# Seven block products in place of eight for two double groups of a feed-forward input

## The chip, the cores and the metric

The kernel runs on one core of one Trainium2 chip. The metric is the time of one execution on the device, in microseconds (us). TensorE (PE) multiplies, VectorE (DVE), ScalarE (ACT) and GpSimd (POOL) work elementwise, SyncE (SP) issues most transfers from HBM.

## The reference

One decoder layer on 256 tokens of 1,024 features, in float32. Before the part that is changed come an attention branch, a recurrent branch, their merge, and cross-attention to 256 memory tokens. What is changed is the last step:

```python
hn = rmsnorm(h, norm_ffn_g[l])
gu = hn @ w_ffn_in[l]                       # 1024 x 5632
h = h + (jax.nn.silu(gu[..., :FFN_HIDDEN]) * gu[..., FFN_HIDDEN:]) @ w_ffn_out[l]   # FFN_HIDDEN = 2816
return rmsnorm(h, final_norm_g)
```

## The kernel before

**Three matmuls for one.** Every float32 operand is cut in two: `hi`, a copy rounded to the format fp32r, and `lo`, the rest. A product is `hi*hi + hi*lo + lo*hi`, three matmuls on TensorE (`mm3t`, lines 238 to 240), added up in PSUM.

**Weight units.** All weights lie in HBM as units of 128 x 2048 numbers (1 MB), in the order `ORDER` in which they are used. `prep` loads a unit into one of two `raw` buffers, ScalarE copies it to `hi` (line 194), and `lo = raw - hi` (line 198) is made by VectorE (1,152 columns) and GpSimd (896 columns, `POOL_COLS`), in two pieces. There are three `hi` and three `lo` buffers, and `nxt` prepares two units ahead of the one in use.

**The feed-forward part.** `FFN_HIDDEN` is worked on in 11 groups of 256 units. A group has two input units `("I", j, kh)`, for the lower and the upper half `kh` of the 1,024 inner features, each with 256 gate columns and 256 value columns, and one output unit `("O", j)`. The order is I, I of group j, then O of group j - 1. For an I unit, `ffn_in` runs for both groups `t` of 128 tokens: four slices of 128 features times three matmuls of 512 columns, so 12 matmuls for each `t`, into the PSUM bank `psi`. After both halves `kh`, `gate` makes silu(gate) * value, where ScalarE and VectorE also apply the token's normalising factor `r`; `turn_hid` transposes the result (four transposes, `hidT`, line 1099) and cuts it (`hid`, lines 285 and 286); an O unit is 24 matmuls into four PSUM banks `acc` that stay for the whole part.

**The turn of h.** While the stage before it (`wo_part`, the output of the cross-attention) still runs, `turn_h2` transposes one quarter of `h` (128 tokens by 512 features) at a time (`h2T`, line 1064), applies the gain (VectorE, line 1066) and cuts it (ScalarE line 1067, GpSimd line 1068). It is turned unscaled; the factor `r` is known later and is used in `gate`. The last quarter is turned between the two `t` of the first I unit, which does not read that quarter yet.

**Who sets the order.** TensorE's instructions stand in the order in which the program writes them. Those of the other engines are put in order by a scheduler when the program is built; the order of the built program is fixed, each engine works strictly through its own, and semaphores hold it where an operand or a buffer is not ready.

Of the kernel before, what the change touches and what calls it, by code (L numbers as in the profile page):

```python
# [24 lines left out]
EPS = 1e-6  # L25
NEG = -1e30
LEAD = 2
POOL_COLS = 896
# [12 lines left out]
V_MIX, V_X, V_MEM, V_FFN, V_HG, V_L0, V_L1 = (8 * i for i in range(7))  # L41


def plan():
    order = []

    def tgroup(name, base):
        return [("T", name, base + c * 512, kh) for c in range(2) for kh in range(2)]

    order += [("T", "w_in", 4096 + c * 512, kh) for kh in range(2) for c in range(2)]  # L50
    order += [("F", "w_in", 3 * 1024 + c * 256) for c in range(4)]
    for base in (5, 2, 0, 1, 6):
        order += tgroup("w_in", base * 1024)
    order += tgroup("w_in", 8 * 1024) + tgroup("w_in", 7 * 1024)
    order += tgroup("w_br_hgrn", 0) + tgroup("w_br_attn", 0)
    order += tgroup("w_out", 0)
    order += [("F", "wkv_x", c * 256) for c in range(4)]
    order += tgroup("wkv_x", 1024)[:2]
    order += [("F", "wq_x", c * 256) for c in range(4)]
    order += tgroup("wkv_x", 1024)[2:]  # L60
    order += tgroup("wo_x", 0)
    for j in range(NF // 2):
        order += [("I", j, 0), ("I", j, 1)]
        if j:
            order.append(("O", j - 1))
    order.append(("O", NF // 2 - 1))
    return order


ORDER = plan()  # L70


def lay(ws):
# [39 lines left out]
def bc(ap, n, axis):  # L113
    shape = list(ap.shape)
    shape.insert(axis, n)
    return ap.unsqueeze(axis).to_broadcast(shape)


def build(tc, A, out):
    nc = tc.nc  # L120
    V, SC, G, PE, SY = nc.vector, nc.scalar, nc.gpsimd, nc.tensor, nc.sync
    with ExitStack() as ctx:
# [3 lines left out]
        cp = pool("cp", 1)  # L126
        wr, wh, wl = pool("wr", 2), pool("wh", 3), pool("wl", 3)
# [114 lines left out]
        def by_k(w, k):  # L242
            return tuple(t.rearrange("p (k c) -> p k c", k=k) for t in w)
# [276 lines left out]
        w = by_k(nxt(), 4)  # L520
# [394 lines left out]
        def add_h(t, c, ps, scale, ssq):  # L915
            d = H[:, t, c * 512:(c + 1) * 512]
            if scale is None:
                V.tensor_tensor(d, ps, d, op=ALU.add)
            else:
                V.scalar_tensor_tensor(d, ps, scale, d, op0=ALU.mult, op1=ALU.add)  # L920
            j = t2b("hjunk")
            SC.activation(j, d, AF.Square, accum_out=ssq[:, t, c:c + 1])

        def rstd2(ssq, name):
            s = small("s2", [2])
            V.tensor_tensor(s, ssq[:, :, 0], ssq[:, :, 1], op=ALU.add)
            return rstd_of(s, name)
# [124 lines left out]
        gfin = big("B4", "gfin", (128, 1024))  # L1052
        SY.dma_start(gfin, A["gfin"].to_broadcast([128, 1024]))
        H2 = big("P2", "H2", (128, 2, 8, 256), F32R)
        h2h, h2l = H2[:, 0], H2[:, 1]
        def wo_part(ps, t, c, kh):
            t_part(ps, wo[2 * c + kh], (oxh, oxl), t, kh)

        def turn_h2(t, c):
            ks, ts = slice(4 * c, 4 * c + 4), slice(t * 128, (t + 1) * 128)  # L1060
            bk = bank("h2T", (128, 4, 128))
            for j in range(4):
                k = 4 * c + j
                PE.transpose(bk[:, j], H[:, t, k * 128:(k + 1) * 128], ident)
            g = t2("h2g", (128, 4, 128))
            V.tensor_tensor(g, bk, bc(gv[:, V_FFN + 4 * c:V_FFN + 4 * c + 4], 128, 2), op=ALU.mult)
            SC.activation(h2h[:, ks, ts], g, AF.Copy)
            G.tensor_tensor(h2l[:, ks, ts], g, h2h[:, ks, ts].bitcast(F32), op=ALU.subtract)

        todo = None  # L1070
        for t in range(2):
            for c in range(2):
                ps = mm.tile([128, 512], F32, name="pso", tag="mm")
                wo_part(ps, t, c, 0)
                if todo:
                    turn_h2(*todo)
                wo_part(ps, t, c, 1)
                add_h(t, c, ps, None, ssq2)
                todo = (t, c)


        ring = ("B7", "B14", "B10", "B11", "B12", "B6")
        X2 = (h2h, h2l)
        hid, acc, two, psi, hm = {}, {}, {}, {}, {}

        def gate(o, t):
            r, ps = two["r"][:, t:t + 1], psi.pop((o, t))
            g = t2("fg", (128, 256))
            SC.activation(g, ps[:, 0:256], AF.Silu, scale=r)  # L1089
            u = t2b("fu", (128, 256))  # L1090
            V.scalar_tensor_tensor(u, ps[:, 256:512], r, g, op0=ALU.mult, op1=ALU.mult)  # L1091
            hm[o, t] = u

        def turn_hid(o):
            bk = mm.tile([128, 2, 256], F32, name="hidT", tag="mm")
            for t in range(2):
                u = hm.pop((o, t))
                for j in range(2):
                    PE.transpose(bk[:, j, t * 128:(t + 1) * 128], u[:, j * 128:(j + 1) * 128], ident)
            hd = big(ring[o % 6], "hid", (128, 2, 2, 256), F32R)  # L1100
            split(bk, hd[:, 0], hd[:, 1])
            hid[o] = hd

        def ffn_in(o, kh, t, w):
            if kh == 0:
                psi[o, t] = mm.tile([128, 512], F32, name="psi", tag="mm")
            t_part(psi[o, t], w, X2, t, kh)
# [11 lines left out]
        def ffn_out(o):  # L1119
            w = by_k(nxt(), 2)  # L1120
            for t in range(2):
                for c in range(2):
                    out_part(o, w, t, c)
# [20 lines left out]
        wa = by_k(nxt(), 2)  # L1144
        wb = by_k(nxt(), 2)
        out_part(n - 1, wa, 0, 0)
        turn_hid(n)
        out_part(n - 1, wa, 0, 1)
# [8 lines left out]


        ssq3 = cp.tile([128, 5], F32, name="ssq3")
        hg3 = {i: big(ring[j], "hg3", (128, 512)) for j, i in enumerate(((0, 0), (0, 1), (1, 0)))}  # L1160
# [95 lines left out]
```

## Time and profile before

| | us |
|---|---|
| median of three executions | 625.4 (624.79 to 625.51) |
| profiled execution, its own time | 625.08 |
| span in its profile, first to last instruction | 623.1 |
| mean granted TensorE clock | 0.998 |
| start of the feed-forward's first matmul | about 431 |
| last matmul | 616.4 |

The span begins with the first instruction and ends with the last; the execution's own time has some 2 us more around it. A row of the timeline gives start and duration in us, the engine, the line of the kernel, the operation, the tiles (output<-inputs) and the count; in square brackets is the idle time of the engine before it and what ended it. A row of the chain of waits gives start, the time until the next piece of the chain, and the instruction. A row of groups gives count | busy time in us, mean duration in ns | idle time before, and what ended it. A row of windows gives the stretch, its length, the busy time and count of TensorE's matmuls, its weight loads, VectorE, ScalarE and GpSimd, then the granted clock, the DMA engines' busy share and GB/s.

### The profile page before, as it was taken

What the parts mean: (1) busy time and instruction counts of PE and PEld (TensorE: products, weight loads), DVE (VectorE), ACT (ScalarE), POOL (GpSimd) and SP (SyncE); (2) the same over time, 40 slices, a digit from 0 to 9 for tenths busy, and PEclk for the clock granted to TensorE, in tenths of its full rate; (3) what the DMA queues carried; (4) which work ended last, traced back from release to release, by engine and by line L of the source; (5) the groups of instructions that cost most, each with busy time, mean ns of one, the idle gap of its engine ahead of it and who ended that gap; (6) DMA issues with size and microseconds to landing.
All of it is one profiled execution on the core that took longest, in us unless ns stands there. A gap on an engine that the chain in (4) does not pass through costs nothing.

```text
span 623.1 us, 8546 instructions
## 1 busy us (share of the span) xinstructions
PE 615.1 (99%) x3153; PEld 513.7 (82%) x3153; DVE 395.6 (63%) x691; ACT 334.1 (54%) x550; POOL 371.5 (60%) x296
## 2 busy tenths in 40 slices
PE   8999999999999999999999999999999999999995
PEld 7888888888877877778888888888888888888884
DVE  7589888979776875748846456754444444444433
ACT  7785554234376866727547556644543344434432
POOL 3888744556544564356857876656655665566553
PEclk9999999999999999999999999999999999999999
DMA  8754553334433333545454544453354455455511
GB/s 346 288 197 149 203 202 136 136 135 147 191 137 135 136 136 136 203 174 191 145 213 189 187 176 178 143 196 135 136 180 175 187 202 184 177 184 198 204 68 68
DMA packets 16890, 107.53 MB, mean 173 GB/s; under 512 B 2000, under 2 KB 2640, under 8 KB 4560
## 3 DMA queue, kind: packets, MB, share of 16 engines
q1 hardware_dynamic: 16128, 106.14, 46.9%
q10 hardware_dynamic: 720, 0.84, 0.4%
q8 instruction: 25, 0.41, 0.3%
q14 instruction: 17, 0.14, 0.1%
HBM read 105.92 MB, written 1.05 MB: 172 GB/s over the span
## 4 chain that ended last, share of the span: by engine, by line
PE 98%; DVE 0%; POOL 0%; issue 0%; POOLq 0%; DVEq 0%
PE pst L238 13%; PE pst L240 13%; PE pst L239 13%; PE psf L259 7%; PE psi L238 6%; PE psi L240 6%; PE psi L239 6%; PE psf L260 4%; PE acc L240 3%; PE acc L238 3%; PE acc L239 3%; PE lp L613 2%; PE psg L514 1%; PE pso L238 1%; PE pso L240 1%; PE pso L239 1%
## 5 line engine op out<-in xcount | busy, mean ns | idle before, releaser
L198 POOL TENSOR_TENSOR lo<-raw,hi 128x448 fp32r<-128x448 f32 x172 | 272.0, 1597 | 181.4 <-ACT hi L194 178.4
L194 ACT ACTIVATE hi<-raw 128x1024 fp32r<-128x1024 f32 (+1 forms) x194 | 196.2, 1037 | 161.1 <-PE pst L240 58.2
L198 DVE TENSOR_TENSOR lo<-raw,hi 128x576 fp32r<-128x576 f32 (+2 forms) x194 | 197.8, 1024 | 127.9 <-ACT hi L194 126.1
L238 PE MATMUL pst<-hi,XX 128*128 128x512 f32 x224 | 90.4, 404 | 0.0
L240 PE MATMUL pst<-hi,XX 128*128 128x512 f32 x224 | 87.4, 390 | 0.0
L239 PE MATMUL pst<-lo,XX 128*128 128x512 f32 x224 | 87.3, 390 | 0.0
L238 PE MATMUL psi<-hi,H 128*128 128x512 f32 x176 | 69.6, 395 | 0.0
L240 PE MATMUL psi<-hi,H 128*128 128x512 f32 x176 | 68.7, 390 | 0.0
L239 PE MATMUL psi<-lo,H 128*128 128x512 f32 x176 | 68.5, 389 | 0.0
L240 PEld LDWEIGHTS pst<-hi,XX 128*128 128x128 f32 x224 | 42.0, 188 | 9.0
L238 PEld LDWEIGHTS pst<-hi,XX 128*128 128x128 f32 x224 | 42.1, 188 | 8.8 <-issue 0.7
L239 PEld LDWEIGHTS pst<-lo,XX 128*128 128x128 f32 x224 | 42.1, 188 | 7.9
L240 PEld LDWEIGHTS psi<-hi,H 128*128 128x128 f32 x176 | 33.0, 188 | 7.1
L239 PEld LDWEIGHTS psi<-lo,H 128*128 128x128 f32 x176 | 33.1, 188 | 6.6
L238 PEld LDWEIGHTS psi<-hi,H 128*128 128x128 f32 x176 | 33.1, 188 | 6.5
L238 PE MATMUL acc<-hi,hid 128*128 128x512 f32 x86 | 33.6, 390 | 0.0
L240 PE MATMUL acc<-hi,hid 128*128 128x512 f32 x86 | 33.5, 389 | 0.0
L239 PE MATMUL acc<-lo,hid 128*128 128x512 f32 x86 | 33.5, 389 | 0.0
L1091 DVE SCALAR_TENSOR_TENSOR fu<-psi,r_h,fg 128x256 f32<-128x256 f32 x22 | 10.6, 483 | 25.1 <-ACT fg L1089 25.1
L1089 ACT ACTIVATE fg<-psi,r_h 128x256 f32<-128x256 f32 x22 | 10.4, 475 | 29.1 <-PE psi L240 29.1
L259 PE MATMUL psf<-H,hi 128*128 128x512 f32 x64 | 22.8, 400 | 0.0
L259 PE MATMUL psf<-XX,hi 128*128 128x512 f32 x64 | 22.6, 396 | 0.0
(336 smaller groups left out, 1199.4 us busy)
## 6 DMA issues: line engine op xcount, KB each, us to landing
raw<-w SPq DMA_DIRECT2D x94, 1024.0 KB, 4.8
raw<-w SPq DMA_DIRECT2D x4, 512.0 KB, 6.5
raw<-w SPq DMA_DIRECT2D x4, 256.0 KB, 4.0
H<-xtok SPq DMA_DIRECT2D x1, 1024.0 KB, 9.6
mraw<-mT SPq DMA_DIRECT2D x1, 1024.0 KB, 4.9
xraw<-xT SPq DMA_DIRECT2D x1, 512.0 KB, 6.5
gfin<-gfin SPq DMA_DIRECT2D x1, 512.0 KB, 3.7
out<-H SPq DMA_DIRECT2D x2, 256.0 KB, 2.0
```

What stands on the lines that cost most here:

```text
L194: SC.activation(hi[:, a], raw[:, a], AF.Copy)
L198: eng.tensor_tensor(lo[:, b], raw[:, b], hi[:, b].bitcast(F32), op=ALU.subtract)
L238: PE.matmul(ps, xh, h, start=first, stop=False)
L239: PE.matmul(ps, xh, l, start=False, stop=False)
L240: PE.matmul(ps, xl, h, start=False, stop=last)
L259: PE.matmul(ps, w[0][:, k, a], X2[:, :, k], start=k == 0, stop=False)
L260: PE.matmul(ps[:, 0], w[1][:, k, a], X2[:, 0, k], start=False, stop=k == 7)
L514: PE.matmul(pss[c][t], z[:, k, t * 128:(t + 1) * 128], ws[c][0][:, k], start=z is Xh and k == 0, stop=False)
L613: PE.matmul(ps[:, j], KS[:, a0 + j], QQ[:, a0 + j], start=True, stop=True)
L1089: SC.activation(g, ps[:, 0:256], AF.Silu, scale=r)
L1091: V.scalar_tensor_tensor(u, ps[:, 256:512], r, g, op0=ALU.mult, op1=ALU.mult)
```

## The change

Only the feed-forward part is changed.

**Seven products.** Groups 3 and 4, and groups 7 and 8, are each taken together. For such a pair q, q + 1 the input product is a 2 x 2 product of blocks: tokens in two halves `t`, inner features in two halves `kh`, and two groups. Eight block products (12 matmuls each) become seven, P1 to P7, in a form after Strassen and Winograd. Sums of token blocks (`token_sums`, tile `SS`) are made once; sums of weight blocks (`load_blocks`, `block`) are made on VectorE by `both`, in two halves of 1,024 columns, in the loaded tiles `b11`, `b12`, `b21` and `b22`, and are then cut like any unit. P1, P6, P5 and P3 add up in one PSUM bank; copies kept on the way (`keep`, ScalarE) are added to other banks by `whole` (VectorE).

**One block sum by a transfer.** For the pair 7, 8 (`BY_DMA`) ScalarE negates block 12, and a transfer issued by GpSimd adds block 22 to it from HBM.

**The order.** `FFN_PLAN` gives 39 units in place of 33: I units of groups 0, 1, 2 and O0; then P1, P2, O1, P6, P7, P5, O2, P3, P4; I units of 5 and 6, O3; then P1, P2, O4, P6, P7, O5, P5, O6, P3, P4; I of 9, O7, I of 10, O8, O9, O10. `prep_u(n + 3)` prepares three units ahead, with a fourth pair of buffers (`px`) beside the three; `raw` stays at two. From the third unit on a unit is cut in one piece. `TURNS` says at which unit `turn_hid` stands, `LOADS` where the four blocks of a pair are asked for.

**The turn.** `h` is now scaled by its factor before it is transposed (`rstd_h2`, `hn`), so `gate` no longer multiplies by `r`. The quarters of `t` = 0 are turned between the two halves of the last `wo_part`. The first four I units run for `t` = 0 alone; then both quarters of `t` = 1 are turned, and the same four units run for `t` = 1.

```diff
+SEVEN = ("P1", "P2", "P6", "P7", "P5", "P3", "P4")
...
+    out = two(0) + two(1) + two(2) + [("O", 0)]
+    out += seven(3, P2=[1], P5=[2]) + two(5) + two(6) + [("O", 3)]
+    out += seven(7, P2=[4], P7=[5], P5=[6])
+    out += two(9) + [("O", 7)] + two(10) + [("O", 8)]
+    return out + [("O", 9), ("O", 10)]
...
+BY_DMA = (7,)
+LOADS = {0: (3,), 14: (7,)}
+TURNS = {4: (0,), 7: (1,), 11: (2,), 18: (3,), 21: (4,), 24: (5,), 26: (6,), 32: (7,), 34: (8,), 35: (9,)}
...
+        def halve(raw, n):
+            if n % 4 == 3:
+                hi, lo = px[:, 0:2048], px[:, 2048:4096]
+            else:
+                hi = wh.tile([128, 2048], F32R, name="hi", tag="hi")
+                lo = wl.tile([128, 2048], F32R, name="lo", tag="lo")
+            pieces = 2 if n < 2 else 1
+            w = 2048 // pieces
+            for c in range(pieces):
+                a = slice(c * w, (c + 1) * w)
+                SC.activation(hi[:, a], raw[:, a], AF.Copy)
+                cut = (c + 1) * w - POOL_COLS // pieces
+                V.tensor_tensor(lo[:, c * w:cut], raw[:, c * w:cut], hi[:, c * w:cut].bitcast(F32), op=ALU.subtract)
+                G.tensor_tensor(lo[:, cut:a.stop], raw[:, cut:a.stop], hi[:, cut:a.stop].bitcast(F32),
+                                op=ALU.subtract)
+            return hi, lo
+
+        def both(out, x, y, op):
+            for i in range(2):
+                a = slice(1024 * i, 1024 * i + 1024)
+                V.tensor_tensor(out[:, a], x[:, a], y[:, a], op=op)
+
+        def load_blocks(q):
+            blk.clear()
+            for key, tag, c in (("22", "B12", (q + 1, 1)), ("12", "B6", (q + 1, 0)),
+                                ("11", "B10", (q, 0)), ("21", "B11", (q, 1))):
+                blk[key] = big(tag, "b" + key, (128, 2048))
+                SY.dma_start(blk[key], A["w"][where[("I",) + c]])
+            if q in BY_DMA:
+                SC.activation(blk["12"], blk["12"], AF.Copy, scale=-1.0)
+                G.dma_start(blk["12"], A["w"][where["I", q + 1, 1]], accum_op=ALU.add)
+            else:
+                both(blk["12"], blk["22"], blk["12"], ALU.subtract)
+
+        def block(name):
+            if name == "P6":
+                both(blk["11"], blk["12"], blk["11"], ALU.add)
+            elif name == "P5":
+                both(blk["12"], blk["22"], blk["11"], ALU.subtract)
+            elif name == "P4":
+                both(blk["21"], blk["21"], blk["11"], ALU.subtract)
+            return blk[{"P1": "11", "P2": "21", "P6": "11", "P7": "12", "P5": "12", "P3": "22", "P4": "21"}[name]]
+
+        def prep_u(upto):
+            while made_u[0] <= min(upto, len(units) - 1):
...
+                if u[0] == "P":
+                    raw = block(u[2])
+                else:
+                    raw = wr.tile([128, 2048], F32, name="raw", tag="raw")
+                    SY.dma_start(raw, A["w"][where[u]])
+                pair[n] = halve(raw, n)
...
+        def product(ps, name, w, first):
+            xh, xl = tokens(name)
+            for k in range(4):
+                for i, (x, z) in enumerate(((xh, w[0]), (xh, w[1]), (xl, w[0]))):
+                    PE.matmul(ps, x[k], z[:, k], start=first and k == 0 and i == 0, stop=k == 3 and i == 2,
+                              skip_group_check=not first)
...
+        def whole(q, t, ps, key):
+            c = t2("fc")
+            V.tensor_tensor(c, ps, kept.pop(key), op=ALU.add)
+            psi[q, t] = c
+            gate(q, t)
...
-        for u in ORDER[at[0]:-2]:
-            if u[0] == "O":
-                ffn_out(u[1])
-                continue
-            _, o, kh = u
-            w = by_k(nxt(), 4)
-            for t in range(2):
-                ffn_in(o, kh, t, w)
-                if (o, kh, t) == (0, 0, 0):
-                    turn_h2(1, 1)
-                    two["r"] = rstd2(ssq2, "h2")
-                if kh == 1:
-                    gate(o, t)
-            if kh == 0 and o:
-                turn_hid(o - 1)
+        prep_u(3)
+        for n in range(4):
+            ffn_in(n, 0)
+        turn_h2(1, hn1)
+        for n in range(4):
+            for q in LOADS.get(n, ()):
+                load_blocks(q)
+            ffn_in(n, 1)
+            if n == 0:
+                token_sums()
+            prep_u(n + 4)
+        for n in range(4, len(units) - 2):
+            for q in LOADS.get(n, ()):
+                load_blocks(q)
+            prep_u(n + 3)
+            for o in TURNS.get(n, ()):
+                turn_hid(o)
+            u = units[n]
+            if u[0] == "I":
+                for t in range(2):
+                    ffn_in(n, t)
+            elif u[0] == "P":
+                ffn_product(n)
+            else:
+                ffn_out(n)
```

More of the change, by code (lines that the diff above doesn't have):

```diff
@@ L70, with ffn_plan, seven, two @@
 ORDER = plan()
+SEVEN = ("P1", "P2", "P6", "P7", "P5", "P3", "P4")
+def ffn_plan():
+    def seven(q, **after):
+        out = []
+        for p in SEVEN:
+            out.append(("P", q, p))
+            out += [("O", o) for o in after.get(p, ())]
+        return out
+    def two(j):
+        return [("I", j, 0), ("I", j, 1)]
+    out = two(0) + two(1) + two(2) + [("O", 0)]
[3 more added lines that the diff above has]
+    return out + [("O", 9), ("O", 10)]
+FFN_PLAN = ffn_plan()
+BY_DMA = (7,)
+LOADS = {0: (3,), 14: (7,)}
+TURNS = {4: (0,), 7: (1,), 11: (2,), 18: (3,), 21: (4,), 24: (5,), 26: (6,), 32: (7,), 34: (8,), 35: (9,)}
 def lay(ws):
@@ L1055, in build @@
         h2h, h2l = H2[:, 0], H2[:, 1]
+        where = {u: i for i, u in enumerate(ORDER)}
+        px = big("P1", "px", (128, 4096), F32R)
+        made_u, pair, blk = [0], {}, {}
+        def halve(raw, n):
[14 more added lines that the diff above has]
+            return hi, lo
@@ L1070, in build, with add_h2, rstd_h2 @@
-        todo = None
+        ssq2 = cp.tile([128, 4], F32, name="ssq2")
+        v2 = cp.tile([128, 2], F32, name="v2")
+        r2 = cp.tile([128, 2], F32, name="r2")
+        h2g = {}
+        def add_h2(t, c, ps):
+            d = H[:, t, c * 512:(c + 1) * 512]
+            V.tensor_tensor(d, ps, d, op=ALU.add)
+            SC.activation(t2b("hjunk"), d, AF.Square, scale=1.0 / 32.0, accum_out=ssq2[:, 2 * t + c:2 * t + c + 1])
+        def rstd_h2(t):
+            V.tensor_scalar(v2[:, t:t + 1], ssq2[:, 2 * t:2 * t + 1], ssq2[:, 2 * t + 1:2 * t + 2], EPS,
+                            op0=ALU.add, op1=ALU.add)
+            G.tensor_tensor(r2[:, t:t + 1], v2[:, t:t + 1], nhalf[:, :1], op=ALU.pow)
+            hn = []
+            for c in range(2):
+                n = t2("hn")
+                SC.activation(n, H[:, t, c * 512:(c + 1) * 512], AF.Copy, scale=r2[:, t:t + 1])
+                hn.append(n)
+            return hn
@@ new lines, in turn_h2 @@
+        def turn_h2(t, hn):
+            for c in range(2):
+                ks, ts = slice(4 * c, 4 * c + 4), slice(t * 128, (t + 1) * 128)
+                bk = bank("h2T", (128, 4, 128))
+                for j in range(4):
+                    PE.transpose(bk[:, j], hn[c][:, j * 128:(j + 1) * 128], ident)
+                g = t2("h2g", (128, 4, 128))
+                V.tensor_tensor(g, bk, bc(gv[:, V_FFN + 4 * c:V_FFN + 4 * c + 4], 128, 2), op=ALU.mult)
+                SC.activation(h2h[:, ks, ts], g, AF.Copy)
+                G.tensor_tensor(h2l[:, ks, ts], g, h2h[:, ks, ts].bitcast(F32), op=ALU.subtract)
+                h2g[t, c] = g
@@ L1071, in build @@
+        hn0 = None
         for t in range(2):
@@ L1117, in out_part, with ffn_in @@
                      (o == 0 or home is not None) and k == 0, k == 1 and o >= NF // 2 - (2 if t and c else 1))
-        def ffn_out(o):
-            w = by_k(nxt(), 2)
+        def ffn_in(n, t):
+            _, o, kh = units[n]
+            if kh == 0:
+                psi[o, t] = mm.tile([128, 512], F32, name="psi", tag="mm")
+            t_part(psi[o, t], by_k(pair[n], 4), X2, t, kh)
+            if kh == 1:
+                gate(o, t)
+        SS = big("P0", "SS", (128, 2, 4, 4, 128), F32R)
@@ new lines, in token_sums, with put @@
+        def token_sums():
+            a11, a12, a21, a22 = (h2g[t, c] for t in range(2) for c in range(2))
+            def put(i, g):
+                SC.activation(SS[:, 0, i], g, AF.Copy)
+                G.tensor_tensor(SS[:, 1, i], g, SS[:, 0, i].bitcast(F32), op=ALU.subtract)
+            V.tensor_tensor(a22, a21, a22, op=ALU.add)
+            s2 = t2("s2", (128, 4, 128))
+            V.tensor_tensor(s2, a22, a11, op=ALU.subtract)
+            put(1, s2)
+            V.tensor_tensor(a21, a11, a21, op=ALU.subtract)
+            put(2, a21)
+            put(0, a22)
+            V.tensor_tensor(a12, a12, s2, op=ALU.subtract)
+            put(3, a12)
@@ new lines, in build, with keep, ffn_product @@
+        bank_of, kept = {}, {}
+        def keep(key, ps, home):
+            SC.activation(home, ps, AF.Copy)
+            kept[key] = home
+        def whole(q, t, ps, key):
[3 more added lines that the diff above has]
+            gate(q, t)
+        def ffn_product(n):
+            _, q, name = units[n]
+            w = by_k(pair[n], 4)
+            key = {"P1": "A", "P6": "A", "P5": "A", "P3": "A", "P2": "B", "P7": "F", "P4": "F"}[name]
+            first = name in ("P1", "P2", "P7")
+            if first:
+                bank_of[key] = mm.tile([128, 512], F32, name="pq" + key, tag="mm")
+            ps = bank_of[key]
+            product(ps, name, w, first)
+            if name == "P1":
+                keep("1", ps, t2("f1"))
+            elif name == "P2":
+                whole(q, 0, ps, "1")
+            elif name == "P6":
+                keep("2", ps, gf[:, 1024:1536])
+            elif name == "P5":
+                keep("4", ps, gf[:, 1536:2048])
+                whole(q + 1, 1, bank_of["F"], "4")
+            elif name == "P3":
+                psi[q + 1, 0] = ps
+                gate(q + 1, 0)
+            elif name == "P4":
+                whole(q, 1, ps, "2")
@@ L1143, in build @@
         n = NF // 2 - 1
-        wa = by_k(nxt(), 2)
-        wb = by_k(nxt(), 2)
+        wa, wb = (by_k(pair[len(units) - 2 + i], 2) for i in range(2))
         out_part(n - 1, wa, 0, 0)
```

65 lines of the change are left out of this document (33 added, 32 removed).

## The prediction, made before the changed kernel ran

> **What bounds the kernel now.** I read the page first: the busy shares, and the shares of the chain that ended last. In these views DVE is VectorE, ACT ScalarE, POOL GpSimd, SP the queue that issues the loads.
>
> ```profile
> span 623.1 us, 8546 instructions
> PE 615.1 (99%) x3153; PEld 513.7 (82%) x3153; DVE 395.6 (63%) x691; ACT 334.1 (54%) x550; POOL 371.5 (60%) x296
> PE 98%; DVE 0%; POOL 0%; issue 0%; POOLq 0%; DVEq 0%
> ```
>
> TensorE is the chain. What a matmul is worth is its pitch in the chain of waits, not its duration in the groups (some 390 ns), since matmuls overlap:
>
> ```profile
> 448.10 0.44 PE hidT L1099 x4
> 464.89 0.44 PE hidT L1099 x4
> ```
>
> These two are one trip of the feed-forward loop apart: 16.79 us hold four transposes and 72 matmuls, so a matmul of 512 columns costs (16.79 - 0.44) / 72 = 0.227 us and a weight unit of 24 matmuls 5.45 us.
>
> Then the question is whether the weights still come fast enough. The timeline of one unit shows how ScalarE makes its upper half (`hi`) and then VectorE (576 of each 1024 columns) and GpSimd (448) the rest (`lo`):
>
> ```profile
> 471.23 2.00 ACT L194 ACTIVATE hi<-raw 128x1024 fp32r<-128x1024 f32 x2
> 472.31 0.76 DVE L198 TENSOR_TENSOR lo<-raw,hi 128x576 fp32r<-128x576 f32 x1 [0.47 <-ACT hi L194]
> 473.26 1.44 DVE L198 TENSOR_TENSOR lo<-raw,hi 128x576 fp32r<-128x576 f32 x1 [0.19 <-ACT hi L194]
> 472.36 3.36 POOL L198 TENSOR_TENSOR lo<-raw,hi 128x448 fp32r<-128x448 f32 x2 [2.88 <-ACT hi L194]
> ```
>
> The same VectorE job takes 0.76 and then 1.44 us, although both have 576 columns. The stretch at 148 us shows why:
>
> ```profile
> 148.86 0.80 DVE L581 TENSOR_TENSOR QK<-QK,Tt 128x512 f32<-128x512 f32 x1
> 149.59 1.77 DVE L583 TENSOR_TENSOR QK<-QK,Tt 128x512 f32<-128x512 f32 x1
> 151.29 2.37 DVE L198 TENSOR_TENSOR lo<-raw,hi 128x576 fp32r<-128x576 f32 x2
> 147.97 1.16 POOL L198 TENSOR_TENSOR lo<-raw,hi 128x448 fp32r<-128x448 f32 x1
> 149.08 1.74 POOL L741 TENSOR_TENSOR ra<-ra,rb__1439 128x512 f32<-128x512 f32 x1
> 150.78 1.59 POOL L198 TENSOR_TENSOR lo<-raw,hi 128x448 fp32r<-128x448 f32 x1
> 431.18 1.29 POOL L1068 TENSOR_TENSOR H<-h2g,H 128x512 fp32r<-128x512 f32 x1
> ```
>
> GpSimd's 448 columns take 1.16 us alone and its 512 columns 1.29 us. At 149.08 it begins 512 columns while VectorE is in L581, and ends at 150.82: 1.29 us after VectorE let go at about 149.5. VectorE's L583, begun at 149.59, ends at 151.36, some 0.55 us after GpSimd let go; then GpSimd, then VectorE. So an operation of VectorE with both inputs in SBUF and one of GpSimd exclude each other and **take turns**; their times add up. Operations that read PSUM do not join in:
>
> ```profile
> 146.72 1.28 POOL L741 TENSOR_TENSOR ra<-ra,rb__1421 128x512 f32<-128x512 f32 x1 [2.68 <-DVE rb__1421 L740]
> 146.74 0.69 DVE L738 TENSOR_TENSOR ra<-pst,Ct 128x512 f32<-128x512 f32 x1
> ```
>
> The Trainium skill, "SBUF — State Buffer", section "Who interferes with whom", says the same: a VectorE instruction with two SBUF inputs and a GpSimd one that reads SBUF block each other for whole instructions. It speaks against this change, which adds such operations and spreads them over less TensorE time; without the rule the sum would be the first rival's. The 0.80, 1.74, 1.77 and 1.59 above agree with it.
>
> **What it removes.** Two groups of units side by side are four weight blocks, 4 x 24 = 96 matmuls; seven block products of 12 are 84. Twice, that is 24 matmuls, and the built program has 2,202 matmuls of 512 columns in place of 2,226. Worth 24 x 0.227 = **-5.4 us**. Transposes stay as many.
>
> **Prices of the new operations.** These rows give the slopes:
>
> ```profile
> 15.84 1.21 DVE L198 TENSOR_TENSOR lo<-raw,hi 128x1024 fp32r<-128x1024 f32 x1
> L198 DVE TENSOR_TENSOR lo<-raw,hi 128x512 fp32r<-128x512 f32 x8 | 5.4, 694 | 0.6 <-ACT hi L194 0.6
> L194 ACT ACTIVATE hi<-raw 128x1024 fp32r<-128x1024 f32 x186 | 191.4, 1055 | 158.8 <-PE pst L240 58.2 <-PE psi L240 32.1 <-PE acc L240 28.1
> L194 ACT ACTIVATE hi<-raw 128x512 fp32r<-128x512 f32 x8 | 4.8, 622 | 2.4 <-DMA x0g<-x0g 1.7 <-DMA raw<-w 0.7
> L286 DVE TENSOR_TENSOR hid<-hidT,hid 128x512 fp32r<-128x512 f32 x11 | 7.5, 685 | 1.4 <-ACT hid L285 1.4
> raw<-w SPq DMA_DIRECT2D x94, 1024.0 KB, 4.8
> ```
>
> A unit is now cut in one piece. ScalarE's 2048 columns: 1.055 + 2 x (1.055 - 0.622) = 1.92 us. VectorE's 1152: 1.21 + 128 x (1.21 - 0.694)/512 = 1.34. GpSimd's 896: 1.16 + 448 x (1.29 - 1.16)/64 = 2.07, at most 2 x 1.16 = 2.32; I take 2.13. Half a block sum (1024 columns) is 1.21 on VectorE. So a unit takes 1.34 + 2.13 = 3.5 us of turns, about as before, but a product uses it up in 12 x 0.227 = 2.7 us.
>
> **The late turn.** Row group 1 of the tokens is now scaled, turned and cut after all four first units have run on group 0, and TensorE stands in its own order behind that turn. Before, the chain ran beside matmuls:
>
> ```profile
> 434.01 0.44 PE h2T L1064 x4
> 434.48 0.69 DVE L1066 TENSOR_TENSOR h2g<-h2T,gv 128x512 f32<-128x512 f32 x1 [1.25 <-PE h2T L1064]
> 435.21 0.63 ACT L1067 ACTIVATE H<-h2g 128x512 fp32r<-128x512 f32 x1 [2.38 <-DVE h2g L1066]
> 435.92 1.29 POOL L1068 TENSOR_TENSOR H<-h2g,H 128x512 fp32r<-128x512 f32 x1 [1.91 <-ACT H L1067]
> ```
>
> `hi` is there 1.83 us and `lo` 3.20 us after the first transpose. Eight transposes cover 0.88: 0.95 us of pause; two matmuls later (2.28) comes `lo`: 0.92 more. Block 12's two halves (2.4 us) stand just ahead on VectorE: 0 to 2.4, I take 0.9, since most of ten microseconds may hide them. Group 0 has the last 12 matmuls of the stage before as cover (4.06 with the transposes and three matmuls, against 3.20), less one GpSimd weight job of 2.13 if it is in front: 0 to 1.3, I take 0.9. Together **+3.7** (1.9 to 5.6).
>
> **The two rounds of seven.** The built program's order on VectorE from P1's weights on is: lo(P1), a `hid` cut, two halves of P6's block, lo(P2), two halves of P4's block, lo(O), lo(P6), a `hid` cut. So P4's block, wanted six units later, stands ahead of the `lo` of the output unit that follows P2. Its seven two-input jobs let GpSimd in between, which has lo(P1), lo(P2), lo(O), lo(P6), lo(P7) ready: 3 x 1.34 + 4 x 1.21 + 5 x 2.13 = 19.5 us to lo(O). The third matmul of O needs the `hid` cut as well, behind lo(P6): + 1.34 + 0.69 = 21.5. In round two the output unit after P7 is ready too, one turn more: 23.7.
>
> TensorE comes to that matmul 2 x 2.73 + 0.45 = 5.9 us after P1's start. How long before P1 is lo(P1) begun? Two `raw` buffers remain, and one is bound for 4.8 (landing) + 1.92 + 1.34 + 2.13 = 10.2 us, or 5.1 us per unit against 5.45 on TensorE: a lead once lost hardly returns. Ahead of round one it is lost: during the late half of the first four units (10.9 us) the turns hold two h2 cuts, four cuts and four sums of tokens (6 x 1.29 + 4 x 0.69) and unit 4: 14.0 us. I take one unit of lead: an output unit with its turn and P1's own jobs, 5.89 + 3.5 = 9.4. Pauses: 21.5 - 15.3 = **+6.2** and 23.7 - 15.3 = **+8.4**. With no lead (3.5) they are 12.1 and 14.3; with three units (over 16.8) none.
>
> Rest of each round: VectorE has five more `lo` (6.7 us), two halves of P5's block (2.4), four 512-column operations on PSUM at 0.69 (2.8) and small gates, some 13 us, and four turns of GpSimd (8.5); TensorE has five products (13.6), the next output unit and most of O (10.4), 24 us. That is close: 0 to 4 us each, I take 2: **+4**.
>
> **The accumulating transfer** puts negation on ScalarE (1.92) and a GpSimd transfer in place of two halves (2.4). The issue waits for the negation, that for a load whose buffer is freed late in round one, and GpSimd's `lo` of the I units queue behind; on SP the next `raw` stands behind two block loads. No row shows such a transfer: from -2.4 to +4.8 (a plain load's time, if GpSimd were held for all of it). I take 0, the I units having room.
>
> **The clock.** Pauses of this length may lower it:
>
> ```profile
> 1.56 3.57 PE warm L335 x15
> 5.13 2.71 PE psg L514 x8
> 8.30 0.92 PE psg L514 x4
> 616.35 0.28 PE L240 MATMUL end<-hi,hid 128*128 128x256 f32 x1
> 616.00:620.00 4.00, 0.63 (x6) 0.43 (x4) 2.51 (x7) 2.32 (x8) 1.84 (x2) 1.00 0.35 131
> 620.00:623.10 3.10, 0.00 (x0) 0.00 (x0) 0.00 (x0) 0.00 (x0) 0.00 (x0) 0.66 0.46 169
> ```
>
> 0.66 over the last 3.1 us is full speed for 1 us and half after: it fell at 621, 4.4 us after the last matmul. Recovery lasted some 5 us (eight matmuls at 0.339, later 0.23), up to 2.5 us lost; as other waits follow, I take 1 for each round: **+2** (0 to 5). The Trainium skill, "TensorE: Matmul & The Clock Gate", section "Why this matters for your kernels", warns of pauses over some 3 us, a free-running window having to be idle. By that the broken pause of round one might escape: +1.
>
> **Sum:** -5.4 + 3.7 + 6.2 + 8.4 + 4 + 2 = +18.9. The profiled execution took 625.1 (span 623.1 and 2.0 around it), the median is 625.4: **644.3 us**.
>
> **Rivals.**
> *The lead holds (faster).* If P1's jobs begin 15.6 (17.8 in round two) us ahead of it, both rounds are covered: 625.4 - 5.4 + 3.7 = 623.7; 620 if the turn is covered too. It would also come so if the big operations did not take turns. For it speaks GpSimd's idle time in this stage:
>
> ```profile
> L198 POOL TENSOR_TENSOR lo<-raw,hi 128x448 fp32r<-128x448 f32 x66 | 110.2, 1688 | 70.6 <-ACT hi L194 70.6
> ```
>
> Against it the turns and the two buffers. Chance 0.07.
> *No lead at all.* 12.1 and 14.3 in place of 6.2 and 8.4: 656, more if the accumulating transfer holds GpSimd. 0.09.
> *A middle,* half a round covered: 626.7 to 634. 0.04. About no change: 0.02. That the matmuls are not saved is excluded by the count.
>
> **Range.** The forecast has 0.78. Half a unit of lead (2.7 us) either way in each round, 5.4, and 4 for the rests below; 5.4 and the transfer's 4.8 above: 634 to 655. A measurement tells 0.2% (1.3 us) from no change. Faster 0.07, same 0.02, slower 0.78 + 0.09 + 0.04 = 0.91.
>
> **What would show it.** Right: TensorE idle only in feed-forward, longest at the output units O1 and O4 behind P2, released by VectorE's `lo`; VectorE's halves there 3.3 us long, each ending 1.2 us after GpSimd's; a pause at the late turn released by ScalarE and then GpSimd. Wrong: P1's `lo` begun over 16 us ahead; halves of 1.2 us beside busy GpSimd; a hold on GpSimd at the accumulating transfer; pauses released by DMA, which would make the loads the cause.

## The result, and the profile after

| | before | after |
|---|---|---|
| median, us | 625.31 (624.79 to 625.51, 4 runs) | 643.75 (643.51 to 645.21, 4 runs) |
| span of the profiled execution, us | 623.1 | 641.7 |
| mean granted TensorE clock | 0.998 | 0.983 |

The ratio is 1.0301 (95% interval 1.0283 to 1.0319): 18.4 us slower, where +18.9 was predicted. The total is right to 0.6 us, but not all of its terms are, and the experiments moved one of them far outside its bounds.

The page after, its first lines, the shares of the chain, and rows of groups and transfers:

```profile
span 641.7 us, 8474 instructions
PE 618.8 (96%) x3129; PEld 513.2 (80%) x3129; DVE 436.7 (68%) x690; ACT 349.9 (55%) x540; POOL 387.7 (60%) x277
PE 85%; POOL 4%; DVE 3%; issue 3%; DMA 2%; ACT 2%; POOLq 0%; DVEq 0%; ACTq 0%
...
L1108 DVE TENSOR_TENSOR b<-b,b 128x1024 f32<-128x1024 f32 x14 | 26.6, 1926 | 0.0
...
b<-w POOLq DMA_DIRECT2D x1, 1024.0 KB, 12.7
```

TensorE fell from 98% of the chain to 85%. The halves of the block sums (L1108) took 1.93 us on average (from 1.21 to 3.15), not 1.21, and the accumulating transfer 12.7 us. What TensorE waited for in the feed-forward part (us in total, times, longest):

```profile
PE acc L263 <- DVE px L1099: 5.7, 1, 5.7
PE acc L264 <- DVE hids L310: 4.3, 2, 3.3
PE psi L262 <- ACT H L1177: 2.1, 1, 2.1
PE hidT L1212 <- DVE fu L1205: 1.2, 1, 1.2
PE psi L264 <- POOL H L1178: 1.0, 2, 0.6
PE psi L262 <- DVE fu L1205: 0.3, 1, 0.3
```

The places are those foretold: VectorE's `lo` and `hid` cuts at O1 and O4, and ScalarE, then GpSimd, at the late turn. VectorE's and TensorE's timeline in round two, from the `lo` of P1 on:

```profile
533.55 2.48 DVE L1099 TENSOR_TENSOR lo<-b,hi 128x1152 fp32r<-128x1152 f32 x1 [0.38 <-ACT hi L1097]
...
536.55 5.60 DVE L1108 TENSOR_TENSOR b<-b,b 128x1024 f32<-128x1024 f32 x2
542.08 3.28 DVE L1099 TENSOR_TENSOR lo<-b,hi 128x1152 fp32r<-128x1152 f32 x1
545.62 5.84 DVE L1108 TENSOR_TENSOR b<-b,b 128x1024 f32<-128x1024 f32 x2
551.71 2.88 DVE L1099 TENSOR_TENSOR px<-raw,px 128x1152 fp32r<-128x1152 f32 x1
...
555.79 0.68 DVE L310 TENSOR_TENSOR hids<-hidT,hids 128x512 fp32r<-128x512 f32 x1
...
542.61 0.47 PE L1266 MATMUL pqA<-hi,H 128*128 128x512 f32 x1
...
554.65 0.80 PE L263 MATMUL acc<-px,hids 128*128 128x512 f32 x1 [5.66 <-DVE px L1099]
556.52 0.79 PE L264 MATMUL acc<-px,hids 128*128 128x512 f32 x1 [1.07 <-DVE hids L310]
```

From the start of lo(P1) to the end of the `hid` cut are 556.47 - 533.55 = 22.9 us (predicted 23.7). P1 itself began at 542.61, so the lead was 9.1 (taken: 9.4). A pair of halves took 5.6 and 5.8 us, since GpSimd's `lo` was let in between; that is 2.8 to 2.9 for a half, where 3.3 was foretold. The same in round one:

```profile
464.58 2.75 DVE L1099 TENSOR_TENSOR px<-b,px 128x1152 fp32r<-128x1152 f32 x1 [0.45 <-ACT px L1097]
...
476.66 3.02 PE L1266 MATMUL pqA<-px,H 128*128 128x512 f32 x12
...
486.27 0.79 PE L264 MATMUL acc<-hi,hids 128*128 128x512 f32 x1 [3.25 <-DVE hids L310]
```

Here the `hid` cut lets TensorE go on at 486.27, 21.7 us after 464.58 (predicted 21.5), but a lead of 12.1 in place of 9.4, and so a smaller pause. The windows show the clock after the three pauses (stretch, its length, busy us and count of TensorE's matmuls, weight loads, VectorE, ScalarE, GpSimd; then granted clock, DMA share, GB/s):

```profile
445.00:452.20 7.20, 6.58 (x16) 4.83 (x16) 3.67 (x4) 2.98 (x4) 5.69 (x4) 0.53 0.10 38
486.00:489.70 3.70, 3.43 (x8) 2.76 (x9) 3.70 (x6) 0.42 (x1) 0.00 (x0) 0.54 0.16 66
551.00:561.40 10.40, 5.67 (x13) 4.11 (x14) 10.40 (x11) 0.42 (x1) 2.39 (x1) 0.51 0.28 101
```

Some 20 us ran at half clock, with some 35 matmuls at 0.43 in place of 0.227 us.

### The profile page after: what moved, and what is told of

Same layout as the page of the kernel before. It is cut to its first block, busy times and chain, and to the rows that moved or that the text cites. A ratio compares the mean times of both kernels' runs of the same rounds, so it can differ in the third digit from the quotient of the medians.

```text
span 641.7 us, 8474 instructions
## 1 busy us (share of the span) xinstructions
PE 618.8 (96%) x3129; PEld 513.2 (80%) x3129; DVE 436.7 (68%) x690; ACT 349.9 (55%) x540; POOL 387.7 (60%) x277
## 4 chain that ended last, share of the span: by engine, by line
PE 85%; POOL 4%; DVE 3%; issue 3%; DMA 2%; ACT 2%; POOLq 0%; DVEq 0%; ACTq 0%
PE pst L262 13%; PE pst L264 13%; PE pst L263 12%; PE psf L283 7%; PE psf L284 4%; PE psi L264 3%; PE psi L262 3%; PE psi L263 3%; PE acc L264 3%; PE acc L262 3%; PE acc L263 3%; DMA raw<-w 2%; PE pqA L1266 2%; POOL lo L1100 2%; PE lp L637 2%
## 5 line engine op out<-in xcount | busy, mean ns | idle before, releaser
L222 POOL TENSOR_TENSOR lo<-raw,hi 128x448 fp32r<-128x448 f32 x106 | 161.0, 1534 | 111.5 <-ACT hi L218 104.9
L218 ACT ACTIVATE hi<-raw 128x1024 fp32r<-128x1024 f32 (+1 forms) x128 | 128.8, 1028 | 94.1 <-PE pst L264 57.2
L222 DVE TENSOR_TENSOR lo<-raw,hi 128x576 fp32r<-128x576 f32 (+2 forms) x128 | 130.0, 1023 | 58.4 <-ACT hi L218 57.2
L1100 POOL TENSOR_TENSOR lo<-raw,hi 128x896 fp32r<-128x896 f32 (+1 forms) x22 | 61.8, 2816 | 30.8 <-ACT hi L1097 30.1
L1099 DVE TENSOR_TENSOR lo<-raw,hi 128x1152 fp32r<-128x1152 f32 (+1 forms) x22 | 32.0, 1454 | 40.2 <-ACT hi L1097 39.2
L1097 ACT ACTIVATE hi<-raw 128x2048 fp32r<-128x2048 f32 (+1 forms) x22 | 38.5, 1758 | 34.6 <-DMA raw<-w 25.0
L262 PE MATMUL psi<-hi,H 128*128 128x512 f32 x80 | 32.9, 411 | 2.4 <-ACT H L1177 2.1
L264 PE MATMUL acc<-hi,hids 128*128 128x512 f32 x78 | 31.3, 401 | 3.3 <-DVE hids L310 3.3
L264 PE MATMUL psi<-hi,H 128*128 128x512 f32 x80 | 32.7, 408 | 1.0 <-POOL H L1178 1.0
L263 PE MATMUL psi<-lo,H 128*128 128x512 f32 x80 | 32.1, 402 | 0.0
L262 PE MATMUL acc<-hi,hids 128*128 128x512 f32 x78 | 31.1, 399 | 0.0
L263 PE MATMUL acc<-lo,hids 128*128 128x512 f32 x78 | 31.0, 397 | 0.0
L1108 DVE TENSOR_TENSOR b<-b,b 128x1024 f32<-128x1024 f32 x14 | 26.6, 1926 | 0.0
## 6 DMA issues: line engine op xcount, KB each, us to landing
b<-w POOLq DMA_DIRECT2D x1, 1024.0 KB, 12.7
```

Source lines behind the costliest of these rows:

```text
L218: SC.activation(hi[:, a], raw[:, a], AF.Copy)
L222: eng.tensor_tensor(lo[:, b], raw[:, b], hi[:, b].bitcast(F32), op=ALU.subtract)
L262: PE.matmul(ps, xh, h, start=first, stop=False)
L263: PE.matmul(ps, xh, l, start=False, stop=False)
L264: PE.matmul(ps, xl, h, start=False, stop=last)
L1097: SC.activation(hi[:, a], raw[:, a], AF.Copy)
```

## The experiments

The theory: VectorE's two-input operations and GpSimd's share one right of way, and with the block sums their sum is too long for the rounds. The rivals: only the place of P4's sum; the loads or the accumulating transfer; the late turn alone; the clock alone. Medians in us; the ratio is to runs of the kernel before on the same chip.

| run | median | ratio (95% interval) |
|---|---|---|
| no_sums | 625.08 | 1.0003 (0.9994 to 1.0012) |
| lo_vector | 626.44 | 1.0025 (1.0014 to 1.0036) |
| before_lo_vector | 625.32 | 1.0000 (0.9991 to 1.0010) |
| sum4_late | 643.89 | 1.0306 (1.0288 to 1.0323) |
| sum4_late_no_transfer | 642.57 | 1.0280 (1.0266 to 1.0294) |
| no_transfer | 634.24 | 1.0136 (1.0118 to 1.0153) |
| two_transfers | 643.31 | 1.0291 (1.0275 to 1.0306) |
| lo_vector_no_transfer | 625.52 | 1.0007 (0.9997 to 1.0017) |
| no_products | 630.00 | 1.0081 (1.0064 to 1.0097) |
| turn_early | 641.14 | 1.0254 (1.0230 to 1.0278) |
| filled | 641.37 | 1.0245 (1.0222 to 1.0268) |
| all_mended | 620.89 | 0.9933 (0.9921 to 0.9946) |

**no_sums: the block sums left out.** The products take the blocks as they were loaded, so what it computes is not the layer.

```diff
         def both(out, x, y, op):
-            for i in range(2):
+            for i in range(0):
```

> Left out: the 14 half block sums on VectorE (1.93 us each beside GpSimd, 27 us in all); the products take the blocks as they were loaded. Turns (VectorE's two-input operations and GpSimd's share one right of way, and their sum is too long for the rounds): the pauses at O1 and O4 (3.5 and 7.5 us), most of the smaller ones behind them (some 3 us) and the half clock after them (some 3.7 us) go, the late turn stays: 625 to 629 us. Order (only the sums that stand ahead of the output unit's lo hurt): the same here. Loads, accumulating transfer or the products themselves as the cause: no more than 3 us gained, 640 to 644.

625.08, 18.7 us less than after. TensorE's waits:

```profile
PE psi L262 <- ACT H L1177: 1.4, 1, 1.4
PE psi L264 <- POOL H L1178: 1.0, 2, 0.6
PE hidT L1212 <- DVE fu L1205: 0.4, 1, 0.4
PE psi L262 <- DVE fu L1205: 0.3, 1, 0.3
```

No wait at an output unit is left. The products, the plan, the loads and the accumulating transfer are still there: without the sums they make no wait at an output unit. 625.08 is what the matmuls save and the late turn costs, one against the other.

**lo_vector: the same work, without GpSimd's part of `lo`.**

```diff
-                cut = (c + 1) * w - POOL_COLS // pieces
+                cut = (c + 1) * w - share // pieces
...
-                G.tensor_tensor(lo[:, cut:a.stop], raw[:, cut:a.stop], hi[:, cut:a.stop].bitcast(F32),
-                                op=ALU.subtract)
+                if share:
+                    G.tensor_tensor(lo[:, cut:a.stop], raw[:, cut:a.stop], hi[:, cut:a.stop].bitcast(F32),
+                                    op=ALU.subtract)
```

with `share` at zero.

> VectorE makes all 2,048 columns of lo in the feed-forward part, GpSimd none. Turns: a unit's lo takes 1.21 + 1024 x 0.516/512 = 2.24 us of right of way in place of 1.34 + 2.13 = 3.47; a round of ten units with seven half sums then needs 10 x 2.24 + 7 x 1.21 = 31 us in place of 43 where TensorE has 36, so the pauses of both rounds and their half clock go and the late turn stays: 623 to 629 us. No turns, VectorE simply has too much to do: each unit adds 0.9 us to the engine that TensorE waits for, ten units a round, 8 to 9 us more in each: 655 or more. Loads or the transfer: unchanged, 641 to 646.

626.44, 17.3 us less than after, although VectorE was given more work (groups of 431 to 600 us, of lo_vector and then of after's GpSimd, 431 to 610):

```profile
L1100 DVE TENSOR_TENSOR lo<-b,hi 128x2048 fp32r<-128x2048 f32 x10 | 22.9, 2286 | 6.4 <-ACT hi L1098 6.4
L1110 DVE TENSOR_TENSOR b<-b,b 128x1024 f32<-128x1024 f32 x14 | 16.9, 1216 | 0.0
```

```profile
L1100 POOL TENSOR_TENSOR lo<-b,hi 128x896 fp32r<-128x896 f32 x10 | 30.4, 3042 | 14.2 <-ACT hi L1097 14.2
```

With GpSimd out of the way a half takes 1.216 us on average in place of 1.926, and VectorE makes all 2,048 columns of a `lo` in 2.29 us, less than GpSimd spent on 896 (3.04, turns included). This is the test that separates turns from an overloaded VectorE, which would have been slower. The Trainium skill ("SBUF — State Buffer", "Who interferes with whom") says that a VectorE instruction with two SBUF inputs and a GpSimd instruction that reads SBUF shut each other out for whole instructions, and the 1.216 against 1.926 bears it out. What the run does not separate is the shorter sum of turns from the `raw` buffers that come free earlier with it.

**before_lo_vector: the same edit without the products.**

```diff
-ALONE = range(9)
+ALONE = list(range(9)) + list(range(64, 97))
```

`ALONE` names the units whose `lo` VectorE makes alone; 64 to 96 are the 33 units of the feed-forward part.

> The kernel before with lo of all feed-forward units on VectorE alone: the same edit as in lo_vector, without the seven products. TensorE is the chain at 98% there and VectorE has room (82 of 184 us busy): no change, 624.5 to 626. If the edit has a worth of its own, apart from the products: below 624.

625.32: no change. GpSimd's share is worth nothing either way where the turns fit into TensorE's time.

**sum4_late: P4's block sum in its written place.**

```diff
+                if late:
+                    tc.keep_in_program_order(ins)
...
-                both(blk["21"], blk["21"], blk["11"], ALU.subtract)
+                both(blk["21"], blk["21"], blk["11"], ALU.subtract, True)
```

> The two halves of P4's block sum are pinned on VectorE behind all that the program writes before them, so that they stand no longer ahead of the output unit's lo; nothing is left out. Order: 2 x 1.21 + one turn of 2.13 = 4.6 us off the pause in each round, and less half clock: 632 to 636 us. Turns as a whole: the pause at O1 and O4 shrinks, but another, later in the round, takes its place since the same work must still fit: 640 to 645, with new waits on VectorE at a product or a hid cut.

643.89, as after. TensorE's waits in it:

```profile
PE hidT L1214 <- DVE fu L1207: 4.5, 1, 4.5
PE acc L264 <- DVE hids L310: 3.5, 4, 1.8
PE pqB L1268 <- DVE fu L1207: 2.2, 1, 2.2
```

The 5.7 at O4 and the 3.3 at O1 are gone, and others have come in their place, the longest at a `hid` turn at 593 us. P4's sum did stand ahead of the output unit's `lo`, as the prediction said; but moving it away gains nothing. Why is seen in sum4_late_no_transfer below.

**no_transfer: block 12 of the second pair summed on VectorE.**

```diff
-BY_DMA = (7,)
+BY_DMA = ()
```

> Block 12 of the second pair is made by two halves on VectorE, as for the first pair; no negation, no accumulating transfer. If the transfer is worth about nothing (the prediction): 642.5 to 645. If it costs, by holding up the raw load issued at 509 us, which took 10.4 us in the trace after in place of the usual 5, and so the pauses of 1.5 and 0.7 us at 525 and 528: 640 to 642.5. If it saves the two halves' time in full (2 x 1.93 us beside GpSimd): 646 to 648.

634.24: 9.5 us less, more than any of the three expectations. The transfers issued from 508.5 to 514 us, median time to landing, in after and then in no_transfer, and the piece of after's chain of waits:

```profile
raw<-w SPq DMA_DIRECT2D x2, 1024.0 KB, 9.8
```

```profile
raw<-w SPq DMA_DIRECT2D x1, 1024.0 KB, 5.4
```

```profile
508.95 10.36 DMA raw<-w
```

The accumulating transfer was issued at 505.63 and took 12.7 us; a raw load issued at 508.95, beside it, took 10.36 where without the transfer the one issued at 509.31 took 5.4. ScalarE and VectorE stood for 9.0 and 8.0 us until it landed, TensorE paused at 525 and 528 us, and round two began with a shorter lead. The negation and the issue on GpSimd did not hold this load up, since it was issued no later than without them. The raw load that follows is hardly the reason either: in no_transfer the loads issued from 499.7 to 509.3 us stand 3.2 us apart and took 4.6 to 5.4 each. The same stretch in no_transfer:

```profile
529.12 2.48 DVE L1099 TENSOR_TENSOR lo<-b,hi 128x1152 fp32r<-128x1152 f32 x1 [0.38 <-ACT hi L1097]
...
541.67 0.48 PE L1266 MATMUL pqA<-hi,H 128*128 128x512 f32 x1
...
548.67 0.50 PE L264 MATMUL acc<-px,hids 128*128 128x512 f32 x1 [0.82 <-DVE hids L310]
```

The lead is 12.6 us in place of 9.1, and the way from lo(P1) to the `hid` cut's matmul is 19.6 in place of 23.0, as fewer turns of GpSimd fell into it. The pause at O4, 7.5 us over the usual pitch in after, is 1.0.

**two_transfers: the transfer doubled.**

```diff
-BY_DMA = (7,)
+BY_DMA = (3, 7)
```

> Both pairs have block 12 made by negation and accumulating transfer: the suspected cost doubled. If the transfer costs by slowing the raw loads beside it (10.4 and 9.2 us in place of 4.8 in the trace after) and these take TensorE's lead ahead of the next round: round one now begins without lead too, its pauses grow from 3.5 us by 3 to 6, less the two halves saved: 645 to 650. If its price of 9.5 us was GpSimd's or ScalarE's queue: one more negation of 1.9 us and 1.1 us of issue, 643 to 646. If loads have slack during the first four units: the two halves ahead of the late turn go, 641 to 643.

643.31, as after. By its number that lies in the range of the queues (643 to 646) and just above that of slack loads, so the trace has to decide. The transfers issued from 431 to 460 us, in two_transfers and then in after:

```profile
raw<-w SPq DMA_DIRECT2D x3, 1024.0 KB, 9.5
b<-w POOLq DMA_DIRECT2D x1, 1024.0 KB, 9.7
```

```profile
raw<-w SPq DMA_DIRECT2D x3, 1024.0 KB, 9.6
```

The raw loads are as slow in after, where no accumulating transfer runs there: they stand beside the loads of the blocks. The added transfer was issued at 442.95, and the first raw load behind it at 455.15, after it had landed, so it delayed no load. The wait at the late turn fell from 2.1 to 1.5 us with the two halves, and a wait of 1.0 us for VectorE's `lo` came up at O1. The run therefore does not double the suspected cost; it shows that a transfer without awaited loads beside it costs about nothing. So the price in after is read from the delay of awaited loads.

**lo_vector_no_transfer: both edits.**

> lo_vector and no_transfer together. If the transfer costs only where the turns have used up the lead: as lo_vector, 625.5 to 627. If it has a price of its own, as no_transfer's 9.5 us would say: 617 to 620. If the two halves on VectorE are now missing to it: 628 to 630.

625.52, 0.9 less than lo_vector, hardly more than the intervals: with room in the turns the transfer costs at most about a tenth of what it costs in after. The two causes are not two sums to be added: 17.3 and 9.5 together would be more than all that was lost.

**sum4_late_no_transfer: both edits.**

> no_transfer and sum4_late together. Order: without the transfer the pauses that are left (1.3 and 3.8 us at O1 and O2 in round one, 1.2 and 0.7 in round two) stand behind P4's halves, and 3 to 5 us of them with their clock go: 628 to 631. Turns as a whole: they move to other places in the rounds, 633 to 636. If the order matters only where the lead is lost: the same, 633 to 636, with the long pause at the hid turn of 593 us (4.8 us in sum4_late) still there.

642.57, outside every expectation: pinning P4's sum costs 8.3 us where the transfer is not there. A row of ScalarE's timeline, TensorE's longest wait, and the chain of waits before that:

```profile
573.12 1.92 ACT L1097 ACTIVATE hi<-b 128x2048 fp32r<-128x2048 f32 x1 [7.04 <-DVE b L1108]
```

```profile
PE hidT L1214 <- DVE fu L1207: 4.6, 1, 4.6
```

```profile
578.38 3.25 POOL px L1100
...
581.64 4.88 DMA raw<-w
...
586.60 1.92 ACT hi L1097
...
588.55 1.36 DVE lo L1099
...
591.05 1.09 DVE fu L1207
```

The late sum held up ScalarE's `hi` of P4 (first fence) and with it the `lo` behind it on GpSimd. That set a `raw` buffer free only at 581.63, the next load was asked for then, and the `fu` that TensorE needed stood on VectorE behind the `lo` of that load. The same happens ahead of round two. There the late sum frees a block buffer late, so that a block load is issued at 509.30, 0.4 us ahead of the awaited raw load:

```profile
b<-w SPq DMA_DIRECT2D x1, 1024.0 KB, 6.9
raw<-w SPq DMA_DIRECT2D x1, 1024.0 KB, 9.0
```

The raw load takes 9.0 us without any accumulating transfer, and P1 of round two begins 5.8 us after its `lo` (540.04 - 534.21), where no_transfer had 12.6. So here a sum done early is better than one done just in time. With P4's sum pinned the transfer costs 1.3 us (643.89 against 642.57), not 9.5: one delay hides the other, and that sum4_late came out like after was such a coincidence.

**no_products: the turn and the plan without the products.**

```diff
-    out += seven(3, P2=[1], P5=[2]) + two(5) + two(6) + [("O", 3)]
...
+    for j in range(2, NF // 2):
+        out += two(j) + [("O", j - 2)]
```

with `LOADS` empty and `TURNS` to match.

> All groups by eight block products (I units), no weight blocks, no block sums, no accumulating transfer; the late turn, the cut in one piece and the lead of three units stay (the sums of tokens are still made, unused). Late turn as in the trace after (0.5 + 2.1 + 0.8 us of pauses and some 2.9 us of half clock): 625 + 6 = 631 us (629 to 633). If the pause there was owed to the first pair's block sums standing ahead of it on VectorE: 625 to 627. If the plan of the units and the lead cost more than the products: 636 or more.

630.00, 5.1 us slower than before. Its waits at the turn are those of no_sums, 1.4 and 1.0 us. The windows behind the turn in no_products and in no_sums:

```profile
446.00:450.20 4.20, 4.10 (x11) 3.23 (x12) 2.85 (x4) 1.26 (x2) 2.73 (x3) 0.59 0.02 4
```

```profile
446.00:450.20 4.20, 4.00 (x18) 3.31 (x19) 2.75 (x4) 1.96 (x3) 2.73 (x3) 1.00 0.08 31
```

Seven matmuls fewer fit in these 4.2 us at the lower clock, 1.6 us. With 2.4 us of waits that makes 4.0 of the 5.1; the rest is not placed.

**turn_early: the turn one unit earlier.**

```diff
-        for n in range(4):
+        for n in range(3):
             ffn_in(n, 0)
         turn_h2(1, hn1)
+        ffn_in(3, 0)
```

> Row group 1 is turned after three of the first four units instead of after all four, so that 12 matmuls (2.73 us) cover its chain (hi 1.83 us, lo 3.20 us after the first transpose). If the late turn's cost is its own and simply adds up: 2.3 + 1.0 us of pauses and 2.9 us of half clock less 0.5 left, 638 to 640 us. If the rounds behind it are held by the sum of turns, TensorE only comes earlier to the next pause and waits longer there: 641 to 643. If the turn is late for another reason (the first pair's loads): 643 to 645, with the same pause.

641.14, 2.6 less. The waits at the turn shrank only from 3.1 to 2.4 us, and those in the rounds grew from 11.5 to 12.4, with the same 5.7 at O4: what TensorE gains at the turn it waits for later. What is left of the gain goes with the clock, whose mean is 0.990 in place of 0.983.

**filled: TensorE kept busy in the pauses.**

```diff
+        def fill(ps, count, add=False):
+            for i in range(count):
+                PE.matmul(ps, zz, h2h[:, 4 * (i % 2):4 * (i % 2) + 4, 0:128], start=not add and i == 0,
+                          stop=i == count - 1, skip_group_check=True)
...
+                if n in FILL:
+                    fill(bank_of["A"], FILL[n], True)
```

`zz` is zeros; 8 matmuls at the late turn, 14 before O1, 24 before O4.

> TensorE is given idle work where it would pause: 8 extra matmuls behind the late turn's transposes, 14 and 24 in front of O1 and O4, adding products with a block of zeros; the result stays. Pauses as such keep their length, only their clock is saved. Clock as a cost of its own: the half clock of 20.5 us (some 6.6 us lost) goes, 637 to 640 us. If what the clock loses is got back as lead for VectorE, so that later waits grow: 641 to 644. If the clock falls for another reason than idle TensorE: the same stretches of 0.5, and slower by what the extra matmuls overshoot, 643 to 647.

641.37. The three windows again:

```profile
445.00:452.20 7.20, 6.32 (x27) 4.92 (x28) 3.84 (x5) 4.35 (x6) 5.44 (x4) 1.00 0.14 56
486.00:489.70 3.70, 3.70 (x18) 3.04 (x17) 3.46 (x5) 0.56 (x2) 0.00 (x0) 1.00 0.00 0
551.00:561.40 10.40, 8.86 (x31) 6.56 (x30) 9.47 (x9) 0.42 (x1) 0.64 (x1) 0.84 0.37 120
```

The clock holds in the first two, so idle TensorE is what lowers it; but only 2.4 us come back. A TensorE at half speed also gives VectorE time, and at full speed it waits for VectorE instead: from the third matmul of O1 to P1 of round two filled takes 55.8 us and after 56.3, though the half clock in that stretch alone had cost after some 1.7.

**all_mended.** lo_vector, no_transfer and turn_early, and

```diff
-                G.tensor_tensor(h2l[:, ks, ts], g, h2h[:, ks, ts].bitcast(F32), op=ALU.subtract)
+                V.tensor_tensor(h2l[:, ks, ts], g, h2h[:, ks, ts].bitcast(F32), op=ALU.subtract)
```

> lo_vector, no_transfer and turn_early together, with the lower part of h (lines 1174 to 1178 after) cut by VectorE in place of GpSimd; nothing left out. Each cost on its own: 24 matmuls less (5.4 us) and neither late turn (no_products: 5.1 us with its clock) nor rounds, with some 1 us of pauses left at O2: 625.3 - 5.4 + 1 = 621 us (619.5 to 622). If a wait takes the place of the late turn (VectorE now has the h cuts, the sums of tokens and every lo): 623 to 627.

620.89, 0.67% faster than before (0.54 to 0.79), and one wait is left:

```profile
PE acc L264 <- DVE hids L310: 0.4, 1, 0.4
```

Of the 5.4 us that the saved matmuls were priced at, 4.3 are seen (3.4 to 4.9 by the interval); 0.4 is this wait, and the rest is not placed.

## Why the prediction was right, and where it was not

- **-5.4 for 24 matmuls.** Close to what all_mended shows: 4.3 us (3.4 to 4.9) and a wait of 0.4.
- **Late turn +3.7.** 2.1 + 1.0 = 3.1 us of waits, in the order ScalarE, then GpSimd. The block sums ahead of the turn make 0.7 of it (in no_sums the wait is 1.4 in place of 2.1), where 0.9 was taken.
- **Round one +6.2.** The 21.5 us of turns were 21.7. Mis-sized is the lead: 12.1 us where 9.4 was taken, so 21.7 - 12.1 - 5.9 = 3.7, and a pause of 3.5 over the usual pitch (3.3 of it a wait). "A lead once lost hardly returns" was too dark: in no_transfer round two begins with 12.6 us, although TensorE had waited for VectorE in round one.
- **Round two +8.4.** 22.9 us and a lead of 9.1: 7.9 by the same sum, 7.5 measured. The size was right and its cause incomplete: without the transfer the lead is 12.6.
- **Accumulating transfer 0 (-2.4 to +4.8).** This step failed. Removing it gives 9.5 us. The prediction looked at who waits for its issue and for its landing, and not at the other loads on the same DMA engines. What the transfer costs, it costs in round two's pause, in the half clock behind it and in the pauses at 525 and 528 us.
- **Rest of the rounds +4.** 1.5 us (the two waits on `fu`), and these vanish with the transfer.
- **Clock +2 (0 to 5).** The direct loss, some 7 us, is far above it; what filled won back, 2.4, is near it, since the rest is given back in waits.
- **The order on VectorE.** The prediction named P4's sum ahead of the output unit as the culprit. The order is as it said, but sum4_late and sum4_late_no_transfer show that changing it gains nothing or loses, since a late sum holds up other work.

So the mechanism (turns that do not fit, at the foretold places) is shown by no_sums and lo_vector, and the close total owes something to errors that cancelled: round one 2.7, the rest 2.5 and smaller ones too high, the clock's direct loss some 5 too low. With the matmuls at their price the measured terms, -5.4 + 3.1 + 3.5 + 7.5 + 1.5 + 7, make 17.2 of 18.4; 1.2 us is not placed.

## What to carry to other kernels

Where two engines take turns, a share given to the slower one lengthens the sum: before moving work off VectorE, count right of way, not busy time, and try giving the slower engine nothing. Price a new transfer by the loads that run beside it and by whether anyone waits for them. A term that is a difference of lead and queue is only as good as the lead, and two such costs do not add: each run that removes one cause moves the wait to the next.

## What the runs showed that was not expected

- An accumulating transfer of 1 MB took 12.7 us (9.7 in the first pair), and plain raw loads issued behind it 9.2 and 10.4 us in place of 4.8. From 505.7 to 518.3 us, while it was under way, the DMA engines moved 284 GB/s; with plain loads alone, from 428 to 440 us, it was 410, at the same busy share of 0.98. A plain block load issued 0.4 us ahead of a raw load also made that one take 9.0 (sum4_late_no_transfer).
- The clock fell to half at 445.3 us in after, 0.6 us behind an idle stretch of 2.1 us at the late turn, and in no_products at 446.7, behind stretches of 1.4 and 0.6, but not in no_sums behind the same 1.4 and 0.6. The mean granted clock of no_sums' ten executions lies between 0.994 and 0.998, so even one and the same kernel can go either way. The Trainium skill ("TensorE: Matmul & The Clock Gate", "Why this matters for your kernels") warns of gaps over some 3 us; by these rows shorter ones, broken by matmuls, can be enough, and the same ones need not be.
- GpSimd's help on `lo` was worth nothing in the kernel before (625.32 against 625.29 on the same chip) and cost 17 us beside the block sums.
